# A fused encoder layer on one core: parts of the folded Fourier map prepared inside the attention, halves of a^T added by the fetching DMA, and split sigmoids placed at their use

## The chip, the core and the metric

The kernel runs on one core of a Trainium2 chip. A core has five engines that each take their own instructions in order: TensorE (PE, matrix products, with weight loads on PEld), VectorE (DVE), ScalarE (ACT), GpSimd (POOL) and SyncE (SP, which here only issues DMAs). Engines meet through semaphores, and 16 DMA engines move data between HBM and on-chip memory. The metric is the device time of one execution in microseconds, the median of three runs.

## What is computed

The reference is one layer of a bidirectional encoder over two requests, a prompt of 256 tokens and a sample of 1024, each with 16 meta tokens ahead of it. Cut to what matters here:

```python
h = rms_norm(x, norm_mix_g)
q, k, v, f, g_attn, g_four = split(h @ w_in)        # gates after a sigmoid
a  = bidirectional_gqa(q, k, v) @ w_attn_o           # 8 query heads, 2 key heads, width 64
fo = fourier_mix(f) @ w_four_o                       # real part of a 2-D DFT, 4 groups of 128 channels
merged = sigmoid(g_attn) * a + sigmoid(g_four) * fo
x = x + merged @ w_out
u = rms_norm(x, norm_ffn_g) @ w_ffn_in
x = x + (silu(gate) * up) @ w_ffn_out
```

All of it is float32, and the output after a final norm drops the meta tokens.

## The kernel before

Every float32 product is made from three products of a shorter float format (fp32r): each operand is split into a high part (a cast on ACT) and a low part (source minus high part, a subtraction on DVE or POOL), and `three` (L217 to L226) issues high by high, high by low and low by high into one accumulator. Tokens lie in ten tiles of 128 (0 to 3 are chunk 0, 4 to 7 chunk 1, both of the sample, 8 and 9 are chunk 2, the prompt), and the 16 meta tokens are carried beside them.

The stages run in this order: norm and transposes; the Fourier map, which is written folded (only half of its positions are computed) into a scratch tensor in HBM, `f_d`, of 516 by 656; q and k/v with rotary positions; attention; the merge; the output projection; and the FFN in and out. The gate product (`gate_gen`) has no place of its own: it is the filler that gives PE work wherever another stage leaves gaps. Its sums go to HBM (`gate`) and come back in the merge as tiles `gt`.

**Attention** goes through 20 units (ten tiles, 8 and 9 first, by two groups of four heads). For each head PE makes the scores `S` (L891), DVE their maximum (L896), ACT the exponential (L903), DVE the scaling by the sum (L908); then, for each block of keys, PE transposes the four heads' probabilities (`pt`, L825), ACT casts the high part (`pT`, L827), DVE makes the low part (L828), and PE multiplies by V (`pv`, L845 and L846), two blocks late. Each finished unit is copied (`ao`, L851, ACT) and stored by SP in two halves into two scratch tensors of a chunk (`a_d`, L855), so that a^T is the sum of the two. In this stage the order on PE, ACT and DVE is the order in which the code is written (`manual_schedule`). The loop that drives it, `build`, gets control back after each head twice, with `slack` true the second time; there it inserts gate work by the table `FILL`. After the last head the units that are left are drained ("drain").

**Beside the drain** before the change: `fourier_parts` (L930 to L970) reads `f_d` back in four blocks of 128x656 (`fr`, L940) and four tail rows (`x64r`; and `y64r`, of a table), casts each half block into a high part (ACT, L959: 8 times 128x328), and subtracts (DVE, L960: 8 times). The tails are three copies each at partitions 0, 32 and 64 (ACT, L966), with a subtraction on POOL (L968) and two memsets. `load_af` (L972 to L1001) then reads the two halves of a^T of a chunk as two tiles (`af`, L987), adds them on DVE (L998, 128x1024, five times), and splits the sum (L208 and L209). The engines outside `manual_schedule`, and all of them after it, are put in order by a scheduler from estimated times; POOL and SP are always put in order so.

**The merge** (L1003 to L1139) goes over eight blocks i of 128 output channels. `load(i)` fetches two Fourier weight blocks (`wmf`) and one attention block (`wma`), and then the six gate blocks `gt`; `need(i)` adds and subtracts the two Fourier blocks on DVE and splits both weights (`wm`, L1036 and L1037); `sigmoid(i)` puts three sigmoids of both gates' columns on ACT (L1046); `fourier(i)` makes the 26 products `fo` (L224 to L226, and L1059 for the tail), copies one (`fst`, ACT, L1070), makes sum and difference (DVE, L1077 and L1078) and multiplies them into the gate in seven pieces (POOL, L1087). Then come, for the chunks 0, 2 and 1, the twelve products `m` of `af` and `wm`, the gate product (DVE, L1125), the sum of the two branches (POOL, L1126), and the split of the result for the output projection (L1128 and L1129). `fourier(i + 1)` stands ahead of the products of i, and `need(i + 2)`, `sigmoid(i + 2)` and `load(i + 3)` follow in the pass of i.

Tiles come from a pool of 27 slots (`Slots`) and 7 triple slots, reused in the order in which they came free, so a new tile's load waits for the last readers of the slot that it gets; a tile may carry the name of the slot's first owner (`pT`, `ml` or `y` for an `fx` or `wm`). Each DMA counts on one of eight semaphores in turn.

Of the kernel before, what the change touches and what calls it, by code (L numbers as in the profile page):

```python
# [17 lines left out]
P = 128  # L18
# [30 lines left out]
KVSTART = 60  # L49
LEAD = (2, 2, 2, 2, 2, 3, 3)  # L50
# [127 lines left out]
class Kernel:  # L178
# [614 lines left out]
    def attention(self, ps, tiles, tag_s, tag_v):  # L793
# [80 lines left out]
        for i, (t, g) in enumerate(units):  # L874
# [56 lines left out]
    def fourier_parts(self):  # L931
# [3 lines left out]
        raw = {}  # L935

        def load(k):
            if k < 4:
                raw[k] = sl.get("fr")
                nc.sync.dma_start(raw[k][:, :NL], self.f_d[k * P : (k + 1) * P, :])  # L940

        load(0)
        load(1)
        xr, yr = sl.get("x64r"), sl.get("y64r")
        for r, src, n in ((xr, self.f_d[512:516, :], NL), (yr, a["w_64"], D)):
            for b in (0, 32, 64):
                nc.sync.dma_start(r[b : b + 4, :n], src)
        slots = self.fparts = [sl.get("fx", F32R, "t") for _ in range(6)]
        y = self.y64 = sl.get("y64", F32R, "t")
        nc.gpsimd.memset(f32(slots[5][:68, HL : 3 * HL]), 0.0)  # L950
        nc.gpsimd.memset(f32(y[:68, :D]), 0.0)
        yield 1
        self.fblock = lambda i: slots[i // 3][:, i % 3 * HL : (i % 3 + 1) * HL]
        for k in range(4):
            r = raw.pop(k)
            for half in range(2):
                src = r[:, half * HL : (half + 1) * HL]
                h, l = self.fblock(4 * k + 2 * half), self.fblock(4 * k + 2 * half + 1)
                nc.scalar.copy(h, src)  # L959
                nc.vector.tensor_tensor(l, src, f32(h), op=ALU.subtract)  # L960
            sl.put(r)
            load(k + 2)
            yield 1
        for r, t, lo in ((xr[:, :NL], slots[5][:, HL : 3 * HL], 32), (yr[:, :D], y[:, :D], 64)):
            for b in (0, 32, 64):
                nc.scalar.copy(t[b : b + 4, :], r[b : b + 4, :])  # L966
            x = slice(lo, lo + 4)
            nc.gpsimd.tensor_tensor(t[x, :], r[x, :], f32(t[x, :]), op=ALU.subtract)  # L968
            yield 1
        sl.put(xr, yr)  # L970

    def load_af(self, c):  # L972
# [8 lines left out]
        def load(i):  # L981
# [3 lines left out]
            loaded[i] = [sl.get("af") for _ in srcs]  # L985
            for src, raw in zip(srcs, loaded[i]):
                nc.sync.dma_start(  # L987
# [829 lines left out]
```

## Time and profile before

| | |
|---|---|
| median of three runs | 1729.08 us (1726.97 to 1729.61) |
| the profiled execution | 1730.22 us, span 1728.5 us |
| PE busy | 1679.2 us, 97% of the span |
| DVE, ACT, POOL busy | 1115.0, 720.5, 272.6 us |
| DMA | 203.03 MB, mean 117 GB/s |

The span is what the profiler recorded, from the first instruction to the last; the run is 1.7 us longer than it. A row of a group gives line, engine, operation, tiles, shapes and count, then busy time, mean nanoseconds, and the engine's idle time ahead with what ended most of it. The rows of stages give the busy time of each engine in a stretch of the span, the clock that TensorE was granted (1.00 is full), the share of the DMA engines' time and the rate.

### The profile page before, as it was taken

What the parts mean: (1) busy time and instruction counts of PE and PEld (TensorE: products, weight loads), DVE (VectorE), ACT (ScalarE), POOL (GpSimd) and SP (SyncE); (2) the same over time, 40 slices, a digit from 0 to 9 for tenths busy, and PEclk for the clock granted to TensorE, in tenths of its full rate; (3) what the DMA queues carried; (4) which work ended last, traced back from release to release, by engine and by line L of the source; (5) the groups of instructions that cost most, each with busy time, mean ns of one, the idle gap of its engine ahead of it and who ended that gap; (6) DMA issues with size and microseconds to landing.
All of it is one profiled execution on the core that took longest, in us unless ns stands there. A gap on an engine that the chain in (4) does not pass through costs nothing.

```text
span 1728.5 us, 25882 instructions
## 1 busy us (share of the span) xinstructions
PE 1679.2 (97%) x9837; PEld 1499.2 (87%) x9837; DVE 1115.0 (65%) x2082; ACT 720.5 (42%) x1411; POOL 272.6 (16%) x307
## 2 busy tenths in 40 slices
PE   7999999999999998989989999999999999999997
PEld 7888879878888886878879999999999998888886
DVE  5423544567777775752479676667666768765685
ACT  6323323456666665631355222222222234444444
POOL 3002333210100113663353000000000000000002
PEclk9999999999999998999999999999999999999999
DMA  5144331322212228624442222322232137653534
GB/s 191 57 147 138 116 116 56 122 74 67 70 57 64 62 66 291 212 92 154 162 155 82 87 68 91 102 91 83 95 103 90 65 123 259 199 186 95 162 97 153
DMA packets 97564, 203.03 MB, mean 117 GB/s; under 512 B 10173, under 2 KB 46169, under 8 KB 97440
## 3 DMA queue, kind: packets, MB, share of 16 engines
q1 hardware_dynamic: 88224, 184.22, 32.5%
q10 hardware_dynamic: 7824, 12.53, 2.0%
q0 software_dynamic: 1392, 4.63, 0.9%
q8 instruction: 77, 1.26, 0.3%
q14 instruction: 47, 0.39, 0.1%
HBM read 143.30 MB, written 58.04 MB: 116 GB/s over the span
## 4 chain that ended last, share of the span: by engine, by line
PE 88%; DVE 5%; issue 2%; ACT 2%; POOL 2%; DMA 1%; SPq 0%; POOLq 0%; ACTq 0%; DVEq 0%
PE i L224 10%; PE i L226 10%; PE i L225 10%; PE o L226 5%; PE o L225 5%; PE o L224 5%; PE g L224 4%; PE pt L825 4%; PE g L226 4%; PE S L891 4%; PE g L225 4%; PE pv L845 2%; PE pv L846 2%; PE wo L226 2%; PE wo L225 2%
## 5 line engine op out<-in xcount | busy, mean ns | idle before, releaser
L1320 ACT CAST w<-wi 128x512 fp32r<-128x512 f32 x168 | 104.0, 621 | 273.2 <-PE i L226 223.9
L224 PE MATMUL i<-A,w 128*128 128x384 f32 x616 | 208.6, 339 | 3.0 <-ACT w L1320 2.6
L226 PE MATMUL i<-A,w 128*128 128x384 f32 x616 | 208.3, 339 | 2.4 <-POOL w L1322 2.4
L225 PE MATMUL i<-A,w 128*128 128x384 f32 x616 | 208.1, 338 | 0.0
L226 PE MATMUL i<-Ah,w 128*128 128x256 f32 x616 | 173.3, 282 | 0.0
L224 PE MATMUL i<-Ah,w 128*128 128x256 f32 x616 | 173.1, 281 | 0.2 <-ACT w L1320 0.2
L225 PE MATMUL i<-Al,w 128*128 128x256 f32 x616 | 173.1, 281 | 0.0
L828 DVE TENSOR_TENSOR pT<-pt,pT 128x512 fp32r<-128x512 f32 x156 | 106.9, 686 | 37.9 <-ACT pT L827 36.7
L827 ACT CAST pT<-pt 128x512 fp32r<-128x512 f32 x156 | 90.8, 582 | 95.0 <-PE pt L825 92.1
L1322 DVE TENSOR_TENSOR w<-wi,w 128x512 fp32r<-128x512 f32 x154 | 105.1, 684 | 29.1 <-ACT w L1320 28.6
L233 POOL TENSOR_SCALAR fin0r<-fin0ss 128x1 f32<-128x1 f32 x1 | 0.8, 788 | 755.3 <-ACT X L241 755.3
L224 PEld LDWEIGHTS i<-A,w 128*128 128x128 f32 x616 | 116.5, 189 | 3.5 <-ACT w L1320 2.8
L896 DVE TENSOR_REDUCE sm<-S 128x1 f32<-128x1040 f32 (+1 forms) x80 | 86.5, 1081 | 50.7 <-PE S L891 47.4
L226 PEld LDWEIGHTS i<-A,w 128*128 128x128 f32 x616 | 116.4, 189 | 3.2 <-POOL w L1322 3.2
L224 PEld LDWEIGHTS i<-Ah,w 128*128 128x128 f32 x616 | 116.1, 188 | 0.6 <-ACT w L1320 0.6
L225 PEld LDWEIGHTS i<-A,w 128*128 128x128 f32 x616 | 116.3, 189 | 0.0
L225 PEld LDWEIGHTS i<-Al,w 128*128 128x128 f32 x616 | 116.3, 189 | 0.0
L226 PEld LDWEIGHTS i<-Ah,w 128*128 128x128 f32 x616 | 116.1, 189 | 0.0
L903 ACT ACTIVATE p<-S,sm 128x1040 f32<-128x1040 f32 (+1 forms) x80 | 80.3, 1003 | 33.7 <-DVE sm L896 27.1
L825 PE MATMUL pt<-ident,p 128*128 128x128 f32 (+1 forms) x624 | 93.4, 272 | 0.0
L226 PE MATMUL o<-wfo,act 128*128 128x512 f32 (+1 forms) x212 | 82.1, 388 | 2.0 <-DVE act L1454 2.0
L225 PE MATMUL o<-wfo,act 128*128 128x512 f32 (+1 forms) x212 | 82.0, 387 | 0.0
(747 smaller groups left out, 4438.4 us busy)
## 6 DMA issues: line engine op xcount, KB each, us to landing
wi<-w_fi SPq DMA_DIRECT2D x48, 512.0 KB, 3.5
wg<-w_g SPq DMA_DIRECT2D x32, 512.0 KB, 3.6
act_d<-sc SPq DMA_DIRECT2D x77, 192.0 KB, 1.9
act<-act_d SPq DMA_DIRECT2D x37, 320.0 KB, 4.1
wfo<-w_fo SPq DMA_DIRECT2D x21, 512.0 KB, 4.1
X<-act_d SPq DMA_DIRECT2D x31, 320.0 KB, 3.4
act_d<-sc SPq DMA_DIRECT2D x77, 128.0 KB, 2.3
gate<-gs ACTq DMA_DIRECT2D x32, 256.0 KB, 3.2
```

Of the source, the lines that this page charges most:

```text
L224: mm(out, sh, mh, start=first and i == 0, stop=False)
L225: mm(out, sh, ml, start=False, stop=False)
L226: mm(out, slo, mh, start=False, stop=last and i == n - 1)
L825: nc.tensor.transpose(pt[:rows, h * P : (h + 1) * P], me.ps4[h][:, col : col + rows], self.ident[:])
L827: nc.scalar.copy(pT[:rows, :512], pt[:rows, :])
L828: nc.vector.tensor_tensor(pT[:rows, 512:1024], pt[:rows, :], f32(pT[:rows, :512]), op=ALU.subtract)
L845: nc.tensor.matmul(me.pv[:], vst, pT[:rows, :512], start=j == 0, stop=False)
L891: nc.tensor.matmul(S[:, base + lo : base + hi], hq, self.kT[seq][g][v][:, lo:hi], start=v == 0, stop=v == 1)
L896: nc.vector.tensor_reduce(nb, S[:, base : base + L], axis=AX.X, op=ALU.max, negate=True)
L903: self.last_exp = nc.scalar.activation(p, S[:, base : base + L], AF.Exp, bias=nb, accum_out=total)
L1320: nc.scalar.copy(w[:, :512], src)
L1322: eng.tensor_tensor(w[:, 512:1024], src, f32(w[:, :512]), op=ALU.subtract)
```

## The change

Four things change, all between the attention's last units and the end of the merge.

- `fourier_parts` is stepped from inside the attention: from the yield with number 121 on (`PARTS = 120`), at each yield with slack (once for a head) one of its 15 steps is issued. Its order is now tails first, then the four blocks with one load in flight, and the eight low parts are made on POOL and not on DVE. Two of the key slots are handed back after tile 9, to make room.
- `load_af` reads the first half of a^T by SP as before, and the second by a DMA from POOL's queue with `accum_op` add into the same tile. The five additions on DVE and five tiles go. The second DMA waits for the first to have landed.
- In the merge the loads of the gates (`load_gates`) are apart from those of the weights (`load`). The weights of i + 3 are now asked for in the pass of i behind `need(i + 2)`, ahead of the products of chunk 1, and the gates of i + 3 at the end of the pass. `need(0)`, `load(1)` and `load_gates(1)` come ahead of the rest of the gate filler (`next(m)` twice).
- Each sigmoid over both gates' columns becomes two: the Fourier half inside `fourier(i)`, ahead of the copy of `fst`, the attention half after `fourier(i + 1)`.

```diff
+PARTS = 120
...
@@ -913,8 +914,10 @@
                 n += 1
             if g == NKV - 1:
                 sl.put(q.pop(t))
+                if t == 9:
+                    sl.put(*self.kv_slots[4:6])
                 if t == tiles[-1]:
-                    sl.put(*self.kv_slots[:6])
+                    sl.put(*self.kv_slots[:4])
...
@@ -932,42 +935,41 @@
-        raw = {}
-
-        def load(k):
-            if k < 4:
-                raw[k] = sl.get("fr")
-                nc.sync.dma_start(raw[k][:, :NL], self.f_d[k * P : (k + 1) * P, :])
-
-        load(0)
-        load(1)
-        xr, yr = sl.get("x64r"), sl.get("y64r")
-        for r, src, n in ((xr, self.f_d[512:516, :], NL), (yr, a["w_64"], D)):
+        slots = self.fparts = {}
+
+        def block(i):
+            if i // 3 not in slots:
+                slots[i // 3] = sl.get("fx", F32R, "t")
+            return slots[i // 3][:, i % 3 * HL : (i % 3 + 1) * HL]
+
+        self.fblock = block
+        block(17)
+        y = self.y64 = sl.get("y64", F32R, "t")
+        tails = [(slots[5][:, HL : 3 * HL], self.f_d[512:516, :], NL, 32), (y[:, :D], a["w_64"], D, 64)]
+        raw = [sl.get("x64r") for _ in tails]
+        for r, (t, src, n, _) in zip(raw, tails):
+            nc.gpsimd.memset(f32(t[:68, :]), 0.0)
             for b in (0, 32, 64):
                 nc.sync.dma_start(r[b : b + 4, :n], src)
-        slots = self.fparts = [sl.get("fx", F32R, "t") for _ in range(6)]
-        y = self.y64 = sl.get("y64", F32R, "t")
-        nc.gpsimd.memset(f32(slots[5][:68, HL : 3 * HL]), 0.0)
-        nc.gpsimd.memset(f32(y[:68, :D]), 0.0)
         yield 1
-        self.fblock = lambda i: slots[i // 3][:, i % 3 * HL : (i % 3 + 1) * HL]
+        for r, (t, _, n, lo) in zip(raw, tails):
+            for b in (0, 32, 64):
+                nc.scalar.copy(t[b : b + 4, :], r[b : b + 4, :n])
+            x = slice(lo, lo + 4)
+            nc.gpsimd.tensor_tensor(t[x, :], r[x, :n], f32(t[x, :]), op=ALU.subtract)
+            sl.put(r)
+            yield 1
         for k in range(4):
-            r = raw.pop(k)
+            r = sl.get("fr")
+            nc.sync.dma_start(r[:, :NL], self.f_d[k * P : (k + 1) * P, :])
+            yield 1
             for half in range(2):
                 src = r[:, half * HL : (half + 1) * HL]
-                h, l = self.fblock(4 * k + 2 * half), self.fblock(4 * k + 2 * half + 1)
+                h, l = block(4 * k + 2 * half), block(4 * k + 2 * half + 1)
                 nc.scalar.copy(h, src)
-                nc.vector.tensor_tensor(l, src, f32(h), op=ALU.subtract)
+                nc.gpsimd.tensor_tensor(l, src, f32(h), op=ALU.subtract)
+                yield 1
             sl.put(r)
-            load(k + 2)
-            yield 1
-        for r, t, lo in ((xr[:, :NL], slots[5][:, HL : 3 * HL], 32), (yr[:, :D], y[:, :D], 64)):
-            for b in (0, 32, 64):
-                nc.scalar.copy(t[b : b + 4, :], r[b : b + 4, :])
-            x = slice(lo, lo + 4)
-            nc.gpsimd.tensor_tensor(t[x, :], r[x, :], f32(t[x, :]), op=ALU.subtract)
-            yield 1
-        sl.put(xr, yr)
 
     def load_af(self, c):
 
@@ -982,22 +984,18 @@
             if i == len(pieces):
                 return
             srcs, j = pieces[i]
-            loaded[i] = [sl.get("af") for _ in srcs]
-            for src, raw in zip(srcs, loaded[i]):
-                nc.sync.dma_start(
-                    raw.v(per, n), src[:][j * per * P : (j + 1) * per * P, :].rearrange("(k p) n -> p k n", p=P)
-                )
+            raw = loaded[i] = sl.get("af")
+            for src, queue in zip(srcs, (nc.sync, nc.gpsimd)):
+                v = src[:][j * per * P : (j + 1) * per * P, :].rearrange("(k p) n -> p k n", p=P)
+                queue.dma_start(raw.v(per, n), v, **({"accum_op": ALU.add} if queue is nc.gpsimd else {}))
 
...
         for i in range(len(pieces)):
             load(i + 1)
-            raws = loaded.pop(i)
-            if len(raws) == 2:
-                r, x = (r[:, :1024] for r in raws)
-                nc.vector.tensor_tensor(r, r, x, op=ALU.add)
-            out.append(self.split(raws[0], 1024, "af", nc.vector, "t"))
-            sl.put(*raws)
+            raw = loaded.pop(i)
+            out.append(self.split(raw, 1024, "af", nc.vector, "t"))
+            sl.put(raw)
             yield 1
 
...
             raws[i] = r, q
+
+        def load_gates(i):
+            if i >= 8:
+                return
             g = gts[i] = [sl.get("gt") for _ in range(3)]
             for half in range(2):
                 for c in range(3):
...
-        def sigmoid(i):
-            if i == 8:
-                return
+        def sigmoid(i, which):
             for c in range(3):
-                g = gts[i][c][:, : 2 * CH_N[c]]
+                n = CH_N[c]
+                g = gts[i][c][:, which * n : (which + 1) * n]
                 with self.tc.issue_after(self.last_exp.ins):
                     nc.scalar.activation(g, g, AF.Sigmoid)
 
...
+                if half == 0:
+                    sigmoid(i, 0)
                 st = sl.get("fst")
                 nc.scalar.copy(st[:, :HL], pp[0][:, :HL])
 
@@ -1090,22 +1093,25 @@
             sl.put(w)
 
         load(0)
+        load_gates(0)
         yield 0
         need(0)
         load(1)
+        load_gates(1)
         for c in range(3):
             self.M[c] = [], []
-        sigmoid(0)
+        yield 0
         yield from fourier(0)
         need(1)
-        sigmoid(1)
         load(2)
+        load_gates(2)
         for i in range(8):
             yield from fourier(i + 1)
             if i == 6:
-                sl.put(*self.fparts, self.y64)
+                sl.put(*self.fparts.values(), self.y64)
             if i == 7:
                 next(then)
+            sigmoid(i, 1)
             w, g3 = wm.pop(i), gts.pop(i)
             for c in (0, 2, 1):
                 gt, n = g3[c], CH_N[c]
...
-                if c == 2 and i < 6:
+                if c == 2:
                     need(i + 2)
-                    sigmoid(i + 2)
+                    load(i + 3)
             sl.put(w)
-            if i < 5:
-                load(i + 3)
+            load_gates(i + 3)
...
@@ -1643,18 +1648,23 @@
             self.mm = ps, "g"
             with self.tc.manual_schedule(engines={E.PE, E.Activation, E.DVE}):
                 later = self.later = deque()
-                for kind, more, slack in self.attention(ps, [8, 9] + list(range(8)), "S", "pv"):
+                parts = self.fourier_parts()
+                for i, (kind, more, slack) in enumerate(self.attention(ps, [8, 9] + list(range(8)), "S", "pv")):
                     while slack and later:
                         later.popleft()()
+                    if slack and i > PARTS:
+                        next(parts, None)
                     gates(self.FILL[kind] + more)
                 while later:
                     later.popleft()()
                 self.later = None
-            early = chain(self.fourier_parts(), self.load_af(0))
+            run_all(parts)
+            early = self.load_af(0)
             next(early)
             next(m)
             for _ in early:
                 gates(1300)
+            next(m)
             gates.rest()
...
```

Line numbers of the changed program are one to six higher than before.

How the rows stand now, at three places. The first is ACT in the last units of the attention, one head and what follows it (`p` is a head's exponentials, `pT` the cast of transposed probabilities, `gs` a gate sum on its way to HBM, `wgh` a gate weight's high part, `ao` a finished unit). Before:

```order
L827 CAST pT_6177<-pt_6280 128x512
L827 CAST pT_6177<-pt_6289 128x512
L851 COPY ao_6298<-pv_6136 128x512
L903 ACTIVATE p_6304,sm<-S_6271,sm 128x1040
L827 CAST pT_6317<-pt_6312 128x512
L827 CAST pT_6343<-pt_6338 128x512
L903 ACTIVATE p_6350,sm<-S_6329,sm 128x1040
L827 CAST pT_6363<-pt_6358 128x512
```

Now, over a similar stretch:

```order
L828 CAST pT_6345<-pt_6340 128x512
L828 CAST pT_6355<-pt_6350 128x512
L852 COPY ao_6360<-pv_6187 128x512
L904 ACTIVATE p_6366,sm<-S_6331,sm 128x1040
L828 CAST pT_6379<-pt_6374 128x512
L969 CAST pT_5933<-fr_6322 128x328
L828 CAST pT_6407<-pt_6402 128x512
L904 ACTIVATE p_6414,sm<-S_6393,sm 128x1040
```

About once a head a cast of `fr`, a block of the folded map, stands between two casts of `pT`; before, no row stood there. On SP the block's load stands behind the stores of the unit (SP of the changed program; `qT` is a tile of queries):

```order
L856 DMA a_d_218<-ao_5970 64x4x128
L856 DMA a_d_219<-ao_5970 64x4x128
L964 DMA fr_6039<-f_d 128x656
L964 DMA fr_6194<-f_d 128x656
L856 DMA a_d_218<-p_6115 64x4x128
L856 DMA a_d_219<-p_6115 64x4x128
L441 DMA wg_6277<-w_g 128x1024
```

Before, that stretch of SP had the stores, `qT` and `wg` alone.

The second place is ACT in the drain, behind the last exponential. Before:

```order
L851 COPY ao_6660<-pv_6503 128x512
L449 CAST wgh_6664<-wg_6508 128x512
L959 CAST fx_6815<-fr_6803 128x328
L827 CAST pT_6676<-pt_6671 128x512
L959 CAST fx_6815<-fr_6803 128x328
L959 CAST fx_6815<-fr_6805 128x328 x2
L827 CAST pT_6693<-pt_6688 128x512
L449 CAST wgh_6664<-wg_6508 128x512
L827 CAST pT_6708<-pt_6703 128x512
L966 CAST y_1034_6817<-y64r_6808 4x1024 x2
L827 CAST pT_6724<-pt_6719 128x512
L456 COPY gs_1_6729<-g_1_6621 128x512
```

and now:

```order
L1047 ACT_TABLE_LOAD
L1047 ACTIVATE gt_6881<-gt_6881 128x512
L828 CAST pT_6794<-pt_6789 128x512
L457 COPY gs_1_6799<-g_1_6690 128x512
L209 CAST afh_6893<-af_6873 128x1024
L458 DMA gate_1_114<-gs_1_6799 128x512
L828 CAST pT_6814<-pt_6809 128x512
L828 CAST pT_6830<-pt_6825 128x512
L1038 CAST wm_6913<-wmf_6876 128x512
L1047 ACTIVATE gt_6882<-gt_6882 128x512
L828 CAST pT_6849<-pt_6844 16x512
L1038 CAST wm_6916<-wma_6879 128x512
```

The casts of `fr`, `x64r` and `y64r` are gone from between the `pT` casts. In their place stand the table load, sigmoids of `gt`, the split of the weights of block 0 (`wm`) and the split of the first half of chunk 0 of a^T (`afh`), which reads the tile that the DMA on POOL's queue adds into.

The third place is the queues of SP and POOL at the end of the drain and the start of the merge. SP before (`gate_0_71` and the like are gate sums, `a_d_216` and `a_d_217` the two halves of chunk 0, 218 and 219 of chunk 1, 220 and 221 of chunk 2):

```order
L855 DMA a_d_218<-ao_6795 64x4x128
L855 DMA a_d_219<-ao_6795 64x4x128
L1024 DMA gt_6827<-gate_2_73 128x256
L940 DMA fr_6838<-f_d 128x656
L940 DMA fr_6850<-f_d 128x656
L987 DMA af_6914<-a_d_216 128x2x512
L987 DMA af_6915<-a_d_217 128x2x512
L987 DMA af_6918<-a_d_216 128x2x512
L987 DMA af_6919<-a_d_217 128x2x512
L987 DMA af_6930<-a_d_220 128x4x256
L987 DMA af_6931<-a_d_221 128x4x256
L987 DMA af_6938<-a_d_218 128x2x512
```

and now:

```order
L856 DMA a_d_218<-ao_6865 64x4x128
L856 DMA a_d_219<-ao_6865 64x4x128
L1026 DMA gt_6925<-gate_1_99 128x512
L1026 DMA gt_6926<-gate_2_100 128x256
L1026 DMA gt_6924<-gate_0_74 128x512
L1026 DMA gt_6925<-gate_1_75 128x512
L1026 DMA gt_6926<-gate_2_76 128x256
L990 DMA af_6973<-a_d_220 128x4x256
L990 DMA af_6979<-a_d_218 128x2x512
L990 DMA af_6982<-a_d_218 128x2x512
```

Before, all ten loads of a^T stood behind the last stores of `ao`. Now the two loads of chunk 0 stand further ahead (19 and 7 rows above the first row shown), and three loads are left behind the last stores and the gates of block 1. POOL now (before it had only the subtractions of `wgl`, the tails' rows and then the rows of `gt`):

```order
L970 TENSOR_TENSOR pT_5933<-fr_6322,pT_5933 128x328
L970 TENSOR_TENSOR pT_5718<-fr_6322,pT_5933 128x328
L451 TENSOR_TENSOR wgl_6478<-wg_6277,wgh_6477 128x512 x2
L451 TENSOR_TENSOR wgl_6735<-wg_6576,wgh_6734 128x512
L990 DMA af_6873<-a_d_217 128x2x512
L451 TENSOR_TENSOR wgl_6735<-wg_6576,wgh_6734 128x512
L990 DMA af_6890<-a_d_217 128x2x512
L990 DMA af_6973<-a_d_221 128x4x256
L990 DMA af_6979<-a_d_219 128x2x512
L1090 TENSOR_TENSOR gt_6881<-fst_7012,gt_6881 128x313
L990 DMA af_6982<-a_d_219 128x2x512
```

The last DMA, for the second half of chunk 1, stands behind a multiplication that reads `fst`, which is there only once the merge's first Fourier sums are copied. On PE the 26 products of `fourier(1)` now stand ahead of the first products `m`, and no longer behind the products `m` of block 0.

More of the change, by code (lines that the diff above doesn't have):

```diff
@@ L1019, in load @@
             raws[i] = r, q
+        def load_gates(i):
+            if i >= 8:
+                return
             g = gts[i] = [sl.get("gt") for _ in range(3)]
@@ L1026, in need @@
         def need(i):
-            if i == 8:
+            if i >= 8:
                 return
```

1 line of the change is left out of this document (removed).

## The prediction

> **What bounds the kernel now.** I read the page first: TensorE is busy 97% of the span, so only its idle time and its slow clock can be won back, or new waits added. Then the windows of the stretch that the change touches, columns PE, PEld, DVE, ACT, POOL busy (with counts), granted clock, DMA share, GB/s:
>
> ```profile
> 540.00:615.00 75.00, 75.00 (x465) 64.51 (x464) 58.73 (x88) 47.36 (x88) 7.72 (x6) 1.00 0.22 61
> ...
> 650.00:660.00 10.00, 10.00 (x64) 8.37 (x62) 4.11 (x7) 8.47 (x12) 3.10 (x3) 1.00 0.70 226
> 660.00:670.00 10.00, 8.05 (x46) 6.88 (x46) 0.86 (x3) 6.73 (x11) 1.77 (x1) 1.00 0.78 226
> 670.00:680.00 10.00, 6.34 (x33) 5.10 (x33) 9.13 (x14) 4.47 (x8) 3.83 (x3) 0.99 1.05 384
> 680.00:690.00 10.00, 7.11 (x20) 5.19 (x21) 8.06 (x9) 2.32 (x3) 7.89 (x7) 0.50 1.03 369
> 690.00:700.00 10.00, 9.75 (x45) 8.05 (x45) 7.72 (x15) 6.58 (x11) 3.43 (x6) 0.83 0.89 306
> 700.00:710.00 10.00, 9.50 (x57) 8.48 (x55) 10.00 (x19) 7.90 (x12) 7.40 (x9) 1.00 0.68 241
> 710.00:720.00 10.00, 9.89 (x57) 8.98 (x58) 8.71 (x17) 5.78 (x10) 7.86 (x12) 1.00 0.41 142
> ...
> 750.00:760.00 10.00, 5.06 (x24) 3.89 (x23) 6.91 (x14) 3.40 (x6) 5.96 (x9) 0.91 0.14 47
> 760.00:770.00 10.00, 10.00 (x55) 9.12 (x55) 4.91 (x12) 3.26 (x6) 7.05 (x11) 0.92 0.39 139
> ```
>
> Two stretches lose time. At the start of the merge PE is idle 1.95 + 3.66 + 2.89 + 0.25 + 0.50 + 0.11 = 9.4 us between 660 and 720, and the clock costs 7.11 x 0.50 + 9.75 x 0.17 = 5.2 us more: 14.6 us. At 750 to 770 it is 4.94 us idle and 5.06 x 0.09 + 10.0 x 0.08 = 1.3 us of clock: 6.2 us. So **20.8 us** is the most that can be won here. In the attention and the drain PE is never idle, so what is put there can only cost.
>
> The waits of PE from 630 to 800 us say for what, in total, times, and the longest:
>
> ```profile
> PE fo L224 <- ACT wm L1036: 7.6, 2, 4.5
> PE m L224 <- ACT afh L208: 2.0, 2, 1.5
> PE m L225 <- DVE afh L209: 1.8, 1, 1.8
> PE m L225 <- DVE afl L209: 1.2, 2, 0.8
> PE fo L226 <- DVE wm L1037: 1.1, 2, 0.6
> ```
>
> The 7.6 are two waits for split weights, 4.5 (the late stretch) and 3.1 (the start); the next three rows are a^T. The chain of waits (start, duration, what) tells what is behind each, in the first stretch and in the late one:
>
> ```profile
> 663.70 0.43 SPq L987
> 664.17 7.98 DMA af<-a_d
> 672.25 1.24 DVE af L998
> 673.51 1.06 ACT y L208
> 674.59 1.03 DVE y L209
> ...
> 694.04 0.16 PE fo L225
> ...
> 699.62 0.23 PE m L224
> ```
>
> ```profile
> 754.27 0.44 ACT fst L1070
> ...
> 757.21 0.63 ACT wm L1036
> 757.86 1.11 DVE wm L1037
> ```
>
> First: a^T is asked for at 663.70, behind the last stores, and needs 7.98 us with DMA shares at 1.05. Late: the cast of weights comes 2.5 us behind a copy of `fst`, after links through POOL that the dots leave out; its `wmf` load had been issued behind the loads of gates, which wait for slots.
>
> **The change part by part.** Durations (min/median/max ns) of what moves, from the rows of its lines, and the groups of 540 to 615 us with the idle time ahead of them:
>
> ```profile
> L959 ACT CAST fx<-fr x8: 459/465/477, 645.7 to 669.8; 128x328 fp32r<-128x328 f32 x8
> L966 ACT CAST y<-y64r x3: 1042/1047/1048, 650.4 to 658.2; 4x1024 fp32r<-4x1024 f32 x3
> L966 ACT CAST fx<-x64r x3: 734/740/742, 653.6 to 656.8; 4x656 fp32r<-4x656 f32 x3
> L968 POOL TENSOR_TENSOR fx<-x64r,fx x1: 1587/1587/1587, 656.9 to 656.9; 4x656 fp32r<-4x656 f32 x1
> L968 POOL TENSOR_TENSOR y<-y64r,y x1: 2469/2469/2469, 659.3 to 659.3; 4x1024 fp32r<-4x1024 f32 x1
> L998 DVE TENSOR_TENSOR af<-af,af x5: 1222/1751/2296, 672.2 to 689.1; 128x1024 f32<-128x1024 f32 x5
> L1046 ACT ACT_TABLE_LOAD  x1: 1283/1283/1283, 661.3 to 661.3; - x1
> ```
>
> ```profile
> L903 ACT ACTIVATION_READ_ACCUMULATOR p<-S,sm 128x1 f32 x17 | 3.3, 194 | 0.0
> L450 POOL TENSOR_TENSOR wgl<-wg,wgh 128x512 fp32r<-128x512 f32 x4 | 5.2, 1289 | 48.6 <-ACT wgh L449 30.9 <-PE pt L825 17.7
> ```
>
> *Parts in the attention.* ACT gets 8 x 0.465 + 3 x 0.740 + 3 x 1.047 = 9.1 us. The 17 heads of 540 to 615 take 75 / 17 = 4.4 us each, and ACT is idle 75 - 47.4 = 27.6 us there, 1.6 a head. One half block a head (0.47) fits. The tails come three in a head: 2.2 and 3.1 us, over the gap by 0.6 and 1.5: the `pT` casts and the exponential behind them on ACT come late by that, and PE, which has no idle time there, loses **about 2.0 us**. The low parts on POOL (128x328; estimate from 128x512: 1.29 x 328/512 = 0.83, eight times) are needed only 50 us later, and DVE, which they could hold up, is idle 16.3 of 75 us. Bounds: 0, and nothing hidden: 9.1 plus the two POOL subtractions (1.6 + 2.5) holding DVE, 13.2. I stay near the lower end since the gap covers most casts.
>
> *The drain.* The tail and block casts leave it; the table load (1.28), sigmoids and the split of the first half of a^T come between `pT` casts, about as much work as leaves. New is a wait: the cast of `afh` stands on ACT ahead of the last `pT` casts, and reads a tile into which POOL's DMA adds, which can start only when SP's load has landed. Behind it wait those casts, so PE's last p·V, then the copy of the last `ao` and SP's last stores. Behind POOL's DMA waits a `wgl` subtraction, for which the gate filler waits. No DMA of this kind is in the trace. Nearest are POOL's plain loads and loads of the same size on SP (KB each, median us to landing):
>
> ```profile
> tabc<-pos_c POOLq DMA_DIRECT2D x4, 520.0 KB, 4.9
> ...
> af<-a_d SPq DMA_DIRECT2D x10, 512.0 KB, 6.8
> gt<-gate SPq DMA_DIRECT2D x16, 256.0 KB, 5.2
> ```
>
> I take 4.9 to 6.8 us for the addition, in the middle of the drain, where the share is 0.70: the cast comes just as the queue reaches it or a little later. **1.0 us**; bounds 0 and 5 (7.98 for the addition, and the last stores as late).
>
> *Start of the merge.* The 3.1 us wait for weights goes: they are split in the drain, no longer behind `fr` casts. The five adds (1.22 to 2.30, some 8 us of DVE, 9.1 of 10 busy there) go. PE has both Fourier blocks ahead of the first `m`: 26 x 0.15 = 3.9 us each, 7.8 us from 668 on (the 8.05 us of 660 to 670 are used up there); then m of a block, 24 x 0.23 + 12 x 0.12 = 7.0 (the narrower chunk 2 taken at half). What is late next is the second half of chunk 1: SP's load, issued about 665, lands at 672 (6.8), POOL's addition then takes 4.9 to 8.0, the split 1.06 + 1.24: 679 to 682. PE wants it at 668 + 7.8 + 2.8 + 1.4 + 1.4 = 681. I leave 1.5 us idle and 0.8 of clock: **2.3 of the 14.6 stay**. Bounds 0, and 10.7: only 3.9 of it hidden, by `fourier(1)`.
>
> The clock held at 0.99 past the 3.1 us wait at the merge's first products, and was at 0.50 only after the idle pieces that followed it (3.66 of 10 us idle, then 2.89). The Trainium skill, TensorE: Matmul & The Clock Gate, "What's actually happening", says the gate goes to half after an idle window of about 3.4 us and back after as long a busy one; the trace agrees, and by the rule alone nothing of the clock's 0.8 would stay.
>
> *Late stretch.* Block 7's weights no longer queue behind slots of gates, and are asked for 7.0 us of `m` and more ahead. The second chain takes 757.86 + 1.11 - 754.27 = 4.7 us from the copy to the end of the split; with a load of 5.2 (the row of `gt` above) ahead of it, that is 9.9 us, and PE has 10.9 us of a block's work (3.9 + 7.0) to do meanwhile. It fits, but only just: **0.7 of the 6.2 stay**; bounds 0 and 6.2. The 24 further sigmoid instructions cost ACT the fixed part of each; ACT is idle 2.1 of 10 us in its fullest stretch of the merge, 700 to 710, and more elsewhere, so nothing.
>
> *Behind the merge* nothing changes but which slot a tile gets. The FFN's groups wait little in all:
>
> ```profile
> L224 PE MATMUL i<-A,w 128*128 128x384 f32 x616 | 208.6, 339 | 3.0 <-ACT w L1320 2.6
> L226 PE MATMUL i<-A,w 128*128 128x384 f32 x616 | 208.3, 339 | 2.4 <-POOL w L1322 2.4
> ```
>
> I take 0, and 2 either way.
>
> **Sum.** 1730.2 (the profiled execution: span 1728.5 and 1.7 outside) - 20.8 + 2.0 + 1.0 + 2.3 + 0.7 = 1715.4. The median of the runs is 1.1 under the profiled one, so **1714.3 us**. All at the best bound and 2 more behind: 1706.3.
>
> **The rivals.**
> 1. *The additions are slow.* If they take twice a load (two passes over the bytes, 2 x 6.8 = 13.6), the drain's cast is 5 us late and chunk 1's second half comes at 665 + 6.8 + 13.6 + 2.3 = 688, 7 us after PE wants it. With 1.5 us of clock for that wait it costs 8.5; of the drain's 5 I count 2, since gate products stand between the turns on PE. Less the 1.0 and 2.3 already counted that is +7.2: 1721.5. For it: DMA shares of 1.03 to 1.05. Against: the loads are spread over 30 us now. A rule that would bring the same: the Trainium skill, SBUF — State Buffer, "SBUF: two separate sides", says a DMA issued from GpSimd's queue can wait for its descriptors while VectorE holds their shared port. No run here shows it; VectorE's rows here are two-input operations of about 1 us, and waits of that length alone would add under 1 us each.
> 2. *The late wait only moves*: another block's weights come late, since `load` now precedes the gates' loads and takes their slots. All but 0.7 of 6.2 back: 1719.8.
> 3. *The change does not do what it says*: the start is bound by the bytes, not by adds or casts. The same bytes pass, so only `fourier(1)`'s 3.9 us is hidden: 10.7 instead of 2.3: 1722.7.
> 4. *No change*: nothing of the attention's additions hidden, 13.2 instead of 2.0: 1725.5, at the edge of what can be told from before.
> 5. *Slower*: ACT waits in the attention for the blocks themselves. Each `fr` cast stands in ACT's queue between `pT` casts, its load on SP stands behind stores that wait for an `ao` copy, and SP's longest such wait is long:
>
> ```profile
> SPq L855 <- ACT ao L851: 49.2, 4, 15.6
> ```
>
> If the tails and the four blocks (six loads) come 4 us after their casts are due, ACT and then PE stand 6 x (4 - 0.4) = 21.6 us: 1736. It decides from about 3 us late each. Against: in the new order two or three heads (9 to 13 us) lie between the `ao` copy and the cast, and a load of that size takes under 5.
>
> **How the numbers follow.** Chances: forecast 0.50, rivals 0.15, 0.08, 0.09, 0.08, 0.10. A measurement of this kernel tells about 0.2%, 3.5 us, from no change: faster is under 1725.6 and slower over 1732.5. Faster 0.50 + 0.15 + 0.08 + 0.09 = 0.82, same 0.08, slower 0.10. A range from 1706 (best bounds) to 1725 (above rival 3) leaves out rivals 4 and 5, 0.18.
>
> **What would show it.** Right: in the changed profile PE's waits for `wm` and `afh` in the merge fall from 13.7 us to under 3, the clock stays above 0.9 in every 10 us of the merge, `m` follows the second Fourier block, and the attention's end moves by 2 us or less. Wrong: PE idle between 550 and 650 (rivals 4, 5), a wait of ACT on `af` or of PE on chunk 1's `afh` above 5 us (rival 1), or a wait of `fo` on `wm` at any later block (rival 2). A granted clock of 0.5 anywhere in the merge would say that idle pieces stay.

## The result, and the profile after

The changed kernel takes 1740.93 us (median of 4 runs, 1740.32 to 1742.17) against 1729.34 us before: ratio 1.0069, 95% interval 1.0052 to 1.0087. It is **slower by 11.6 us**; 1714.3 was forecast, and the whole range lay below. The profiled execution is 1740.38 us with a span of 1738.6. Where the span went, by the first start on PE of each stage:

| stretch of the span, us | before | forecast | after |
|---|---|---|---|
| to the last `S` of the attention | 634.4 | +2.0 | 639.3 (+4.9) |
| drain, to the first `fo` | 33.3 | +1.0 | 40.1 (+6.8) |
| merge, to the first `wo` | 109.8 | -17.8 | 107.0 (-2.8) |
| from there to the end | 950.9 | 0 | 952.2 (+1.2) |
| span | 1728.5 | -14.8 | 1738.6 (+10.1) |

The windows of the changed kernel, columns as before:

```profile
540.00:615.00 75.00, 71.56 (x427) 60.91 (x426) 56.24 (x82) 51.51 (x93) 16.91 (x14) 0.98 0.27 76
...
650.00:660.00 10.00, 9.87 (x60) 8.33 (x58) 2.37 (x4) 5.66 (x10) 3.94 (x3) 1.00 0.79 214
660.00:670.00 10.00, 5.70 (x26) 5.10 (x27) 4.70 (x8) 4.44 (x8) 1.20 (x1) 0.66 0.93 269
670.00:680.00 10.00, 10.00 (x56) 8.28 (x55) 2.86 (x5) 7.04 (x15) 0.00 (x0) 1.00 1.00 299
680.00:690.00 10.00, 10.00 (x62) 9.32 (x60) 3.32 (x8) 3.52 (x8) 6.37 (x10) 1.00 1.07 353
690.00:700.00 10.00, 4.42 (x16) 3.35 (x16) 3.38 (x5) 4.07 (x7) 1.80 (x5) 0.66 1.12 260
700.00:710.00 10.00, 5.38 (x21) 4.22 (x20) 9.30 (x16) 6.18 (x13) 7.37 (x9) 0.83 0.66 223
710.00:720.00 10.00, 10.00 (x50) 9.20 (x49) 8.20 (x15) 6.81 (x14) 6.87 (x9) 0.83 0.48 147
...
760.00:770.00 10.00, 7.84 (x40) 6.70 (x39) 6.18 (x13) 4.07 (x9) 5.91 (x9) 0.90 0.09 26
770.00:780.00 10.00, 10.00 (x53) 8.88 (x52) 5.77 (x11) 3.48 (x5) 8.16 (x10) 0.93 0.43 157
```

In 540 to 615, in the attention, PE now has a hole of 3.44 us, and in the drain one of 4.4; in both places it had none. At the merge's start the hole is as large as before, only later: 690 to 720 holds 10.2 us of idle and 4.1 of slow clock (4.42 x 0.34 + 5.38 x 0.17 + 10.0 x 0.17), 14.3 against 14.6. The late stretch, now 760 to 780, keeps 2.16 of idle and 1.5 of clock, 3.6 of 6.2. Note 690 to 700: the DMA engines are busy throughout (1.12), at 260 GB/s, where shares of 1.03 to 1.05 gave 369 to 384 before.

PE's waits from 540 to 800 us:

```profile
PE fo L225 <- ACT wm L1038: 4.9, 2, 3.3
PE m L225 <- ACT afh L209: 4.7, 1, 4.7
PE pt L826 <- DVE pT L829: 4.4, 1, 4.4
PE S L892 <- ACT p L904: 3.4, 1, 3.4
PE m L226 <- DVE afl L210: 1.6, 2, 1.4
```

What stands behind three of them: ACT's timeline at the attention's wait, ACT's and DVE's in the drain, and the chain of waits at the merge's start:

```profile
563.34 3.18 ACT L957 CAST pT<-x64r 4x1024 fp32r<-4x1024 f32 x3 [0.40 <-ACT gs L457]
...
568.97 1.13 ACT L904 ACTIVATE p<-S,sm 128x1040 f32<-128x1040 f32 x1 [1.84 <-POOL pT L959]
```

```profile
663.15 1.04 ACT L209 CAST afh<-af 128x1024 fp32r<-128x1024 f32 x1 [2.91 <-DMA af<-a_d]
```

```profile
663.22 0.43 DVE L1034 TENSOR_TENSOR wmf<-wmf 128x256 f32<-128x256 f32 x1 [7.06 <-DMA gt<-gate]
663.56 0.68 DVE L829 TENSOR_TENSOR pT<-pt,pT 128x512 fp32r<-128x512 f32 x1
```

```profile
676.79 1.45 SPq L990
...
678.34 15.44 DMA af<-a_d x2
693.80 1.05 ACT afh L209
```

In the attention an exponential waits for POOL. In the drain ACT's cast of `afh` waits for the adding DMA, and a low part of `pT` waits on DVE behind an operation that reads block 0's weights and could start only at 663.22 (the profile names a gates' load as the last event; in run 13, below, the same wait is named for the weights). In the merge two transfers of one tile, one behind the other, take 15.44 us: SP's, until POOL can issue its own at 683.38, and POOL's addition, until 693.8. ACT's cast for chunk 2 stands idle for 10.27 us of that, and PE waits 4.7 us for it.

### The profile page after: what moved, and what is told of

Read it like the earlier page. It is cut to its first block, busy times and chain, and to the rows that moved or that the text cites. A ratio compares the mean times of both kernels' runs of the same rounds, so it can differ in the third digit from the quotient of the medians.

```text
span 1738.6 us, 25878 instructions
## 1 busy us (share of the span) xinstructions
PE 1683.6 (97%) x9837; PEld 1504.4 (87%) x9837; DVE 1102.8 (63%) x2069; ACT 724.0 (42%) x1435; POOL 277.3 (16%) x320
## 4 chain that ended last, share of the span: by engine, by line
PE 86%; DVE 4%; DMA 3%; issue 2%; POOL 2%; ACT 2%; SPq 0%; POOLq 0%; ACTq 0%; DVEq 0%
PE i L227 10%; PE i L225 10%; PE i L226 10%; PE o L227 5%; PE o L226 5%; PE o L225 5%; PE g L225 4%; PE g L227 4%; PE pt L826 4%; PE g L226 4%; PE S L892 4%; PE pv L846 2%; PE pv L847 2%; PE wo L226 1%; PE wo L225 1%
## 5 line engine op out<-in xcount | busy, mean ns | idle before, releaser
L826 PEld LDWEIGHTS pt<-ident,p 128*128 128x128 f32 (+1 forms) x624 | 73.1, 135 | 15.0 <-DVE pT L829 4.6
L227 PE MATMUL o<-wfo,act 128*128 128x512 f32 (+1 forms) x212 | 82.1, 388 | 2.1 <-DVE act L1459 2.1
```

The source lines that it names most:

```text
L227: mm(out, slo, mh, start=False, stop=last and i == n - 1)
L826: nc.tensor.transpose(pt[:rows, h * P : (h + 1) * P], me.ps4[h][:, col : col + rows], self.ident[:])
```

## The experiments

Fourteen kernels were timed beside the kernel before. The table gives, in us, the median, the ratio to the kernel before with its interval, and three starts on PE in the profile.

| run | time | ratio | last `S` | first `fo` | first `wo` |
|---|---|---|---|---|---|
| the change | 1740.9 | 1.0069 (1.0052 to 1.0087) | 639.3 | 679.4 | 786.4 |
| 1 two loads | 1725.5 | 0.9969 (0.9956 to 0.9981) | 639.4 | 673.3 | 773.7 |
| 2 adding DMA alone | 1737.5 | 1.0039 (1.0024 to 1.0054) | 634.5 | 667.8 | 784.2 |
| 3 parts alone | 1724.2 | 0.9963 (0.9950 to 0.9976) | 639.4 | 673.9 | 773.2 |
| 4 merge's part alone | 1730.4 | 1.0002 (0.9992 to 1.0011) | 634.5 | 667.8 | 777.3 |
| 5 tails held | 1722.9 | 0.9953 (0.9938 to 0.9968) | 635.1 | 669.0 | 768.9 |
| 6 plain DMA on POOL's queue | 1726.9 | 0.9981 (0.9972 to 0.9990) | 640.2 | 674.7 | 776.0 |
| 7 packed slots | 1723.7 | 0.9959 (0.9944 to 0.9974) | 639.7 | 673.8 | 769.7 |
| 8 held, packed, one cast | 1718.9 | 0.9928 (0.9911 to 0.9944) | 634.9 | 668.8 | 768.4 |
| 9 add onto zeros | 1737.5 | 1.0042 (1.0027 to 1.0057) | 641.9 | 683.4 | 789.8 |
| 10 chunk 0 after the drain | 1747.7 | 1.0098 (1.0081 to 1.0115) | 640.1 | 673.9 | 791.7 |
| 11 sum on DVE | 1713.7 | 0.9902 (0.9887 to 0.9917) | 634.5 | 668.2 | 760.8 |
| 12 run 8 with the merge's part | 1720.5 | 0.9939 (0.9924 to 0.9954) | 634.9 | 669.3 | 766.6 |
| 13 series without adding | 1735.3 | 1.0030 (1.0018 to 1.0042) | 640.1 | 677.6 | 780.9 |
| 14 run 11 with the merge's part | 1713.5 | 0.9904 (0.9888 to 0.9921) | 634.6 | 668.9 | 761.4 |

**Which part costs.** Theory T: the adding DMAs are the loss. Rival R: the gates and sigmoids moved ahead are. Run 1 takes the adding DMA out of the change, runs 2 to 4 are each part alone on the kernel before.

```diff
-            raw = loaded[i] = sl.get("af")
...
-                queue.dma_start(raw.v(per, n), v, **({"accum_op": ALU.add} if queue is nc.gpsimd else {}))
+            loaded[i] = [sl.get("af") for _ in srcs]
...
+                nc.vector.tensor_tensor(r, r, x, op=ALU.add)
```

That is run 1; run 2 is the reverse edit on the kernel before, and runs 3 and 4 are the hunks of the change's diff that belong to the parts and to the merge.

> The change, but both halves of a^T are loaded by SP into two tiles and added on DVE, as before. Theory T (the adding DMAs are the loss: each starts only when the first half has landed, and what waits for it on ACT and on SP in the drain holds everything behind): the drain's 4.4 us idle of PE and the 4.7 us wait for afh at 694.9 go, the last loads of a^T are issued some 8 us earlier in the drain; time 1722 to 1728. Rival R (the gates' loads and sigmoids that were moved ahead are the loss): ACT still waits for gt in the drain and a^T still stands behind the gates on SP; time 1736 or more.

> The kernel before with the adding DMA alone. T: two transfers in series of 7 to 9 us each where there was one of 8 and an add of 1.2 to 2.3: PE waits for afh and afl in the merge's first 30 us 5 to 10 us longer than before; time 1734 to 1740. R: no loss without the early gates, since five DVE adds and five tiles go; 1727 to 1731.

> The kernel before with the parts of the Fourier map in the attention alone. T: the attention ends 4.8 us later (the exponential that waits for POOL at 569 us is there again), and the merge's first wait for wm (3.1 us) goes; time 1729 to 1733. A rival that the parts are free in this surrounding: 1724 to 1727.

> The kernel before with the merge's part alone (loads of weights and gates apart, sigmoids split, block 0 and 1 asked for ahead of the rest of the gate filler). T: the late wait of 4.5 us for wm goes or shrinks to 2; the drain is unharmed, since no adding DMA is there; time 1722 to 1727. R: gates ahead of a^T on SP and sigmoids between casts on ACT stop the drain by 4 us or more; 1731 to 1736.

T holds for the adding DMAs: without them the change is 1725.5, so they cost 15.4 us in it, and 7.3 alone (1737.5 - 1730.2). Run 1 has every early gate load and sigmoid, and its drain is 33.9 us long (673.3 - 639.4), 0.6 over before, so R falls. What T said of the other two parts did not come. It put the parts alone at 1729 to 1733, and they take 1724.2. It put the merge's part alone at 1722 to 1727, and it takes 1730.4, no change; on top of the parts (run 1 against run 3) it brings nothing either.

The parts alone bring 6.1 us, though their attention is 4.9 us longer: the merge is 99.3 us long and not 109.8. From 670 to 720 PE then idles 0.83 + 2.32 + 0.58 = 3.7 us at a clock of 1.00, where before the start of the merge lost 14.6. So the parts alone win most of what the forecast sought at the merge's start, and with the adding DMAs it is lost again.

**The attention's 4.9 us.** Run 5 is run 3 with the raw tiles of the tails handed back later.

```diff
             nc.gpsimd.tensor_tensor(t[x, :], r[x, :n], f32(t[x, :]), op=ALU.subtract)
-            sl.put(r)
...
+        sl.put(*raw)
```

> The kernel before with the parts in the attention alone, and the two raw tiles of the tails handed back only at the end of the parts. If the 3.4 us of PE idle at 570 us are the exponential waiting, through the slot that a raw tile left, for POOL's subtraction of 2.3 us: idle under 1.5 us there, the clock back to 1.00 in 540 to 600, time 3 to 5 us under the parts alone (1724.2), 1719 to 1721. If ACT's three casts of 1.05 us in one head are the loss by themselves: idle of 2.5 us or more stays, 1723 to 1725.

PE's waits from 540 to 900 us in run 5, and in run 8 the row of the tails' casts, now one each:

```profile
PE S L892 <- ACT p L904: 1.6, 1, 1.6
```

```profile
L956 ACT CAST pT<-x64r x2: 751/899/1047, 558.8 to 563.9; 68x656 fp32r<-68x656 f32 x1, 68x1024 fp32r<-68x1024 f32 x1
```

The wait falls from 3.4 to 1.6, and the last `S` comes 4.3 us earlier. So the exponential's tile took the slot that the raw tile had left, and had to wait for the POOL subtraction (2.34 us) that still read it. What was left of the wait goes with the single casts in run 8, where PE is busy throughout 540 to 600. Of the 4.3 us only 1.3 show in the time of run 5 (two medians of 4 and 5 runs; 2.4 by the spans), less than the 3 to 5 expected. The first `wo` still comes 4.3 us earlier, so the rest was lost behind the merge; that was not followed up.

**What about the adding DMA costs.** Run 6 loads the second half plainly on POOL's queue into its own tile. Run 9 adds onto zeros, so nothing is in series, and its a^T lacks the first half; run 13 has the change's program order and waits, with only the adding taken out, so its a^T is the second half alone. Run 10 moves chunk 0 out of the drain.

```diff
+            loaded[i] = [sl.get("af") for _ in srcs]
+            for src, raw, queue in zip(srcs, loaded[i], (nc.sync, nc.gpsimd)):
...
+                queue.dma_start(raw.v(per, n), v)
...
+            nc.vector.tensor_tensor(r, r, x, op=ALU.add)
```

> The change, but POOL's DMA loads the second half into a tile of its own with no adding and no wait for the first, and DVE adds the two as before. If the loss is the series (the second transfer starts when the first has landed, and every reader waits for both) the time is that of two loads on SP, 1724 to 1728. If it is POOL's queue itself (its descriptors, its 1.3 us an issue, its place behind other POOL work) the loads still land 9 us or more after the issue and ACT stands in the drain: 1734 or more.

```diff
+            raw, other = sl.get("af"), sl.get("af")
+            nc.vector.memset(raw[:, :1024], 0.0)
+            for src, dst, queue in zip(srcs, (other, raw), (nc.sync, nc.gpsimd)):
```

> The change, but the first half is loaded by SP into a tile that nobody reads, and POOL's adding DMA goes onto a tile that DVE has zeroed, so it waits for no other transfer (a^T lacks its first half). Same bytes, same queues, the addition kept, only the series gone. If the series is the loss: landing of 6 to 7 us as the plain load on that queue, time 1724 to 1729. If the addition itself is slow: landing of 9 us or more with nothing to wait for, ACT stands in the drain, time 1731 to 1738.

```diff
-            early = self.load_af(0)
-            next(early)
...
-            for c in (2, 1):
+            for c in (0, 2, 1):
```

> The change, with the loads and the split of chunk 0 of a^T taken behind the last gate products instead of in the drain. If the drain's loss is the cast of afh in ACT's queue and the tile behind it that SP waits for: the first fo comes at 673 to 675 (679.4 in the change, 673.3 with two loads), and the wait for a^T moves into the merge, time 1733 to 1739. If it is the gates and sigmoids in the drain: first fo at 677 or later.

```diff
-                queue.dma_start(raw.v(per, n), v, **({"accum_op": ALU.add} if queue is nc.gpsimd else {}))
+                queue.dma_start(raw.v(per, n), v)
```

> The change with the adding taken out of POOL's DMA: it writes plainly into the same tile, still after SP's load has landed, so a^T is its second half alone. The instructions and their order on every engine are those of the change. If the adding itself is the price (the DMA engines of that queue were busy 16.8 us for 2.62 MB against 7.8 plain): landing falls from 10.4 to 6 to 7.5 us, issue from 1.3 to 0.7, first fo at 674 to 676, time 1726 to 1731. If the series is the price: landing falls little, first fo at 677 or later, time 1735 to 1741.

POOL's `af` DMAs in the change (count and issue, min/median/max in ns; then the time to landing), and the DMA queues' view of 645 to 705 us (packets, MB, share of the 16 engines):

```profile
L990 POOL DMA_DIRECT2D af<-a_d x5: 1179/1291/1687, 654.1 to 686.3; - x5
DMA to landing us min/median/max: 6.9/10.4/13.4
```

```profile
q0 software_dynamic: 1616, 2.62, 25.9%
```

and in run 13, with the same order and no adding, the same two views:

```profile
L990 POOL DMA_DIRECT2D af<-a_d x5: 704/747/815, 654.9 to 684.8; - x5
DMA to landing us min/median/max: 6.0/7.3/7.8
```

```profile
q0 software_dynamic: 720, 2.62, 12.5%
```

The same bytes take 1616 packets instead of 720, and 60 x 0.259 = 15.5 us of all 16 engines' time instead of 7.5. Landing goes from 10.4 to 7.3 and the issue from 1.29 to 0.75 us. That part is worth 1740.9 - 1735.3 = 5.7 us; the other 9.8, to run 1, is the series and the order and queue that come with it. In run 13 landing and issue are as the one guess had them, first `fo` and time as the other: the price is shared. The 9.8 should not be read as the larger share, for part of it lies outside the drain and the merge. From the last `S` to the first `wo`, the change takes 147.1 us, run 13 140.8 and run 1 134.3, so the two shares there are alike, 6.3 and 6.5.

POOL's queue as such is fast: run 6 (landing 5.3 to 8.2 us) comes within 1.4 us of two loads on SP. Run 9's time tells little of the merge, because its zeroing on DVE also moved the issues (the last at 687.4, behind a split on DVE), and its profiled execution is 3.4 us above its median, so its starts in the table are late. Its landing of 8.3 us with nothing to wait for, though under the 9 of the guess, fits a slow addition. Its drain tells more; ACT's, DVE's and PE's rows there:

```profile
663.59 1.04 ACT L209 CAST afh<-af 128x1024 fp32r<-128x1024 f32 x1 [6.61 <-DMA af<-a_d]
```

```profile
657.93 0.70 DVE L1036 TENSOR_TENSOR wmf<-wmf 128x256 f32<-128x256 f32 x1 [0.74 <-DMA wmf<-w_mb]
```

```profile
PE pt L826 <- DVE pT L829: 5.7, 1, 5.7
```

The addition is issued at 654.7, waits for no other transfer, and its reader starts at 663.6, 8.9 us later. Block 0's weights had landed by 657.9, so here the cast of `afh`, with the `pT` casts behind it, holds PE by itself, and for longer than in the change. In the drain, then, a slow addition is enough, without the series.

Run 10 has its drain back (33.8 us), so what is fetched there is what stops it, but it is 6.7 us slower than the change, far from its guess: its merge is 117.8 us long against 107.0, since the a^T that is not fetched in the drain is waited for in the merge.

**The late stretch.** Run 7 frees a slot a block; run 8 joins runs 5 and 7 and the single cast; run 11 moves the sum of the branches from POOL to DVE in run 8; run 12 is run 8, and run 14 run 11, with the change's merge part.

```diff
-            nc.sync.dma_start(q[:, :512], a["w_ma"][i])
+            nc.sync.dma_start(q[:, 512:1024], a["w_ma"][i])
-            g = gts[i] = [sl.get("gt") for _ in range(3)]
+            g = gts[i] = [sl.get("gt"), sl.get("gt"), q]
```

> The kernel before with the parts alone, and the attention block's raw weights loaded into the unused half of the slot of chunk 2's gates, one slot fewer per block. If the late wait (4.3 us at about 755, a cast of wm behind POOL's multiplications) is a slot that fst held, it shrinks under 1.5 us: 1717 to 1721. If it is the length of the chain ACT to POOL to ACT whatever the slot, it stays: 1723 to 1725.

```diff
-            nc.gpsimd.memset(f32(t[:68, :]), 0.0)
+            nc.gpsimd.memset(r[:68, :n], 0.0)
...
-            for b in (0, 32, 64):
-                nc.scalar.copy(t[b : b + 4, :], r[b : b + 4, :n])
+            nc.scalar.copy(t[:68, :], r[:68, :n])
```

> Parts alone, raw tiles held, packed slots, and each tail cast in one instruction over 68 partitions instead of three over 4 (the raw tile is zeroed instead of the target). If the three are independent: 1724.2 less 4.5 less 4.5, 1714 to 1717. If the time gained in the attention is lost again behind DMA in the first 30 us of the merge: 1718 to 1721.

```diff
-                nc.gpsimd.tensor_tensor(v, v, gt[:, :n], op=ALU.add)
+                nc.vector.tensor_tensor(v, v, gt[:, :n], op=ALU.add)
```

> The fastest version so far (1718.9) with the sum of the two branches on DVE instead of POOL (three operations a block, 3.2 us of POOL for some 2 us of DVE). If POOL's chain holds the last blocks (waits of 2.4 and 0.9 us and a clock of 0.86 near 750): these go, 1715 to 1717. If DVE, full in 680 to 690, becomes the bound at the start: no change or slower, 1719 to 1723.

> The fastest version so far (1718.9) with the change's merge part as well (weights and gates loaded apart, split sigmoids, the first two blocks prepared ahead of the rest of the gates). If preparing ahead takes the 4.4 us wait for wm at 669 us: 1714 to 1717. If it only adds small sigmoids and moves the wait, as it did alone (1730.4 against 1730.2): 1718 to 1721.

> Fastest version so far (1713.7: parts early, raw tiles held, one cast a tail, packed slots, sum on DVE) with the change's merge part as well. If the merge part pays once POOL's chain is off the path: the 3.5 us wait for wm at the merge's start goes, 1709 to 1712. If it only shifts loads: 1713 to 1716.

PE's waits from 660 to 800 us for split weights, of runs 3, 7 and 11 in this order, the window 720 to 750 of run 11, and two rows of run 1, of DVE and ACT:

```profile
PE fo L225 <- ACT wm L1038: 7.4, 3, 4.3
```

```profile
PE fo L225 <- ACT wm L1039: 4.0, 3, 1.7
```

```profile
PE fo L225 <- ACT wm L1038: 3.5, 1, 3.5
```

```profile
720.00:750.00 30.00, 29.94 (x171) 26.94 (x170) 22.94 (x46) 11.77 (x21) 9.25 (x17) 1.00 0.23 72
```

```profile
741.46 0.43 DVE L1038 TENSOR_TENSOR wmf<-wmf 128x256 f32<-128x256 f32 x1 [2.60 <-DMA wmf<-w_mb]
```

```profile
752.99 0.62 ACT L1042 CAST wm<-wmf 128x512 fp32r<-128x512 f32 x1 [1.66 <-POOL gt L1094]
```

In run 1, which has the weights asked for early, the late wait is still 4.4 us. The last block's Fourier weights are read by DVE at 741.46 and so had landed, but ACT's cast of them starts at 752.99, behind a multiplication on POOL. So the loads were not what held it. A free slot a block (run 7) shortens the late wait from 4.3 to 1.5 us (the 1.7 of its row stands at 686). Its merge is 3.4 us shorter than run 3's (95.8 against 99.3), yet the time gains nothing that can be told (1723.7 against 1724.2, with 1717 to 1721 expected): the gain is lost behind the merge, and that was not followed up. In run 8 the three edits together do not add up: 1718.9, inside the second guess, with a wait of 4.4 us for `wm` at the merge's start and a merge of 99.6 us.

With POOL relieved in run 11 the late wait is gone; the 3.5 us of its row stand at the merge's start. POOL is busy 9.25 of 30 us in 720 to 750, and 18.6 in run 8, and the merge is 7 us shorter (92.6 against 99.6); 1713.7 is better than either guess. The chain through POOL's multiplications and sums was the bound; that the slot is its link to the weights is read from run 7, and not shown alone. The merge's part of the change adds nothing in any company (run 14 against 11: 1713.5 and 1713.7). In run 14 the wait for `wm` at the merge's start is down to 0.7 us, but waits for `fst` and a^T come in its place, and the merge is as long (92.5 us). Runs 11 and 14 are the fastest, 1% below the kernel before.

## Why the prediction was wrong

- *What bounds the kernel, and the 20.8 us.* The reading held. Run 11 wins some 17 us, in the two stretches named.
- *Parts in the attention, 2.0 us.* Measured 4.9: 3.4 of idle PE and 1.4 of clock (0.97 of full in 550 to 600). The working counted ACT's casts, and took POOL's subtraction to be needed only 50 us later. Its result was, but its source tile was handed back, and the next exponential got the slot. Held, the wait is 1.6, near the 1.5 of the casts; the clock is then 1.00. The Trainium skill, TensorE: Matmul & The Clock Gate, "What's actually happening", puts the fall after an idle window of some 3.4 us. The traces agree in part: here 1.6 us cost no clock, 3.4 us showed 0.97 over 50 us, and a wait of 4.4 us in run 8 showed 0.66 over 10. But it also came behind shorter waits: in run 7 the clock was 0.83 in 750 to 760 behind a late wait of 1.5 us. So the prediction's "the trace agrees" was too strong: in the kernel before, the clock held through the wait of 3.1 us, as the Trainium skill would have it, and then fell to 0.50 in 680 to 690, where no wait of PE since had been above 1.9 us.
- *The drain, 1.0 us.* Measured 6.8. I weighed the cast of `afh` on ACT alone. It waited 2.9 us, to 663.15, but the weights of block 0 landed no sooner: DVE's first operation on them ended its wait at 663.22, and stood ahead of a `pT` low part. Both were transfers in flight with the adding DMA (654 to 663), and with two plain loads DVE's operation came at 656.2 and the drain lost 0.6 us. Run 9 shows that the cast alone is enough: there the weights were in by 657.9, and PE still lost 5.7 us. Whether the weights alone would hold PE in the change stays open. The term that was mis-sized is the addition: 4.9 to 6.8 us were taken, and it landed after 9.1 (issued at 654.09, read at 663.15).
- *Start of the merge, 2.3 of 14.6 us left.* **This is the step that failed most**: 14.3 stayed, and these 12.0 are about half of the 24.9 us by which the span missed. Three terms were off. The series took 15.44 us, where I had 6.8 + (4.9 to 8.0): a plain load's latency stood for an addition that lands in 10.4. SP's load for chunk 2 came at 676.8 and that for the second half of chunk 1 at 679.3, where I had 665; of this, 11.7 us is only that the first `fo` came as much later. And chunk 2, wanted by PE before chunk 1, was the one that came late; I had worked out chunk 1 only.
- *Late stretch, 0.7 of 6.2 left.* 3.6 stayed. The reason given, weights queued behind slots of gates, was wrong: run 1 has them early and waits 4.4 us. It is POOL's chain (run 11): in run 1 the cast came 11.5 us after its weights were there.
- *The rivals.* Rival 1 had the mechanism, at a chance of 0.15 and a price of 7 us against some 15 in the runs; it stayed on the faster side because I never let it meet the attention's loss, and counted 2 us for a drain that lost 6.8. Its sign came, a wait of ACT on `af` above 5 us (10.27). Rival 2's wait stayed at its old place, and not for its reason. Rival 3 falls: in run 3 the same bytes pass, and 3.7 us stay. Rival 4 falls: the attention lost 4.9 and not 13.2. Rival 5 had slower by another way: ACT waits for no load of `fr` in the attention. The Trainium skill, SBUF — State Buffer, "SBUF: two separate sides", offered descriptors held up by VectorE for POOL's queue; run 6 gives no sign of it, with plain loads landing in 5.3 to 8.2 us.

## What to carry to other kernels

An addition made by a DMA was not a free addition here: price it as a second transfer behind the first, and, as in this case, at about twice the DMA time a byte, and ask what else is in flight then. When a tile is handed back early in a pool that reuses slots in order, find the next owner: its writer inherits the wait for the slowest reader of the old one. And when a wait is to be removed, follow its chain through every engine, for the queue that looks guilty may only stand next to the engine that is.

## What the hardware showed

A DMA of 512 KB that adds took 1616 / 5 = 323 packets where a plain one took 144, 3.1 us of all 16 engines' time instead of 1.5 (15.5 / 5 and 7.5 / 5), and 1.2 to 1.7 us to issue on POOL instead of 0.7 to 0.8. A cast of 4 partitions costs ACT what one of 68 does (4x1024: 1.05 us, 68x1024: 1.05), so three casts of four rows each were three times the price of one cast over all of them.
